# A two-block transformer kernel: x and mem loaded as feature tiles, tap spectra and norm steps in another order, sparse attention's products over all 128 rows

## Chip, core and metric

One core of a Trainium2 chip runs the whole program in one launch. The metric is the device time of one execution in microseconds; times are medians of several runs, and a profile is one further execution.

## What is computed

Two blocks of a model run one after the other on 256 tokens of 1024 features, in float32.

```python
def first_block(x, mem, ...):
    h = x
    h = h + hybrid_mixer(rmsnorm(h, norm_mix_g), ...)      # state-space scan and stick-breaking attention
    h = h + memory_cross_attention(rmsnorm(h, norm_xa_g), mem, norm_mem_g, ...)
    h = h + sqrelu_mlp(rmsnorm(h, norm_ff_g), w_ff1, w_ff2)
    return rmsnorm(h, final_g)

def conformer_conv(h, ...):                                # second block, first layer
    a, gate = jnp.split(h @ w_pw1 + b_pw1, 2, axis=-1)
    u = causal_dwconv_2(a * jax.nn.sigmoid(gate), w_dw, b_dw)   # width 31
    u = jax.nn.silu(layernorm(u, ln_g, ln_b))
    return u @ w_pw2 + b_pw2

def nsa_attention(h, ...):                                 # second block, second layer
    # 16 query heads, 4 key heads of 64; three branches, gated and added:
    # compressed keys (15 blocks), selected blocks, sliding window
    return o @ w_out
```

Each layer of the second block ends in a gated feed-forward net (`conv_ffn`, width 2816). With 256 tokens every block is selected and the window covers everything before a token, so the selected and the window branch are both causal softmax attention with keys of their own.

## The kernel before

Activations lie with features on the partitions: a tile of two feature blocks is 128 partitions by 2 by 256 tokens. Every weight streams once from one long array, in chunks of 128 by 1024 (512 KB), in the order of `_plan`. `chunk` (L351) loads one into one of five `raw` buffers (SP issues the DMA, L348), ScalarE writes `hi`, the rounded fp32r part (L356), and VectorE the rest `lo` (L357); there are seven buffers of each. A product with a weight is three fp32r products: hi by hi, hi by lo, lo by hi (`mm_b`, `mm_a`; all products are issued at L309). Activations are split likewise (`Norm.feed`: ScalarE at L529, VectorE at L530). A product of plain fp32 tiles takes two passes and stands in the profile as two instructions.

The code is straight-line Python. The framework takes each engine's instructions in the written order as far as their operands and buffers are there by its own estimate of times, and adds the waits; so an instruction that is ready may go ahead of one written earlier. Buffers come from pools by tag: `c4` (4 KB a partition, NC4 of them), `t2` (2 KB, eight), PSUM banks `acc` (four), `up` (two), `ms` (two).

**Start.** `load_tokens` (L317) reads mem, and later x, with tokens on the partitions, in four pieces each, the rows of a piece 1 KB long. `turned` (L582) transposes a piece on TensorE (four transposes at L587, PSUM tile `ps_t`), VectorE copies the result (L596 for mem, L609 for x, the latter into `hT`), and `feed` makes the split parts. SP issues in the order mem 0, the first constants `ct`, mem 1, the first vectors `vt`, mem 2, the first chunk of w_xv, mem 3, and further chunks. mem's products come first (w_xv, PSUM `ps_v`, L555), then x is transposed, then w_xk (`ps_xk`, L613), then the mixer's projections.

**Conv module (L974 to L1128).** The depthwise convolution of width 31 is done in the frequency domain: `dft_load` brings matrices and taps, `tap_spectra(m)` (L993) makes the taps' spectra with products over 32 rows (PSUM `ps_sp`, copied by ScalarE at L998), `project` (L1000) makes one 512-wide half of the value (`a`) or gate (`g`) projection out of four chunks (`ps_pw`), `forward` and `back` go to the spectrum and back (`ps_f`, `ps_y`). `normed(t)` (L1061) does the layer norm of 128 tokens: statistics, a reciprocal root, and the scaling of two halves b = 0, 1 of 512 features, b = 1 on VectorE (L1072) and b = 0 on ScalarE (L1074). `feature(p, t)` (L1077) transposes them back (`ps_t`, p = 0, 1 from half 0), `activated` applies silu, and the `pw` products follow.

**Sparse attention (L1170 to L1461).** Its steps are letters in `NSA_ORDER` (L30), written out by hand: p, n, r project, norm and rotate a group of query heads, w makes the softmax weights of a pair of heads (`n_weights`, L1319), t transposes them, c and u do the compressed branch, o forms the output (`n_out`, L1398). Keys are in `kh` (hi, for both halves of the partitions) and `kl` (lo). A query tile `qq` holds hi on the 64 partitions of its own half and lo on the other 64, so one product with `kh` over 128 rows gives hi by hi and lo by hi; the product with `kl` uses 64 rows (L1336). A third, bf16 product adds the mask. VectorE takes the minimum (L1338), ScalarE the exps (L437 in `fn`), GpSimd scales them by gates and sums (L1346). In `n_out` the compressed values `vbd`, of 64 rows for each pair, are multiplied first (L1401), then the two other branches' transposed weights.

Of the kernel before, what the change touches and what calls it, by code (L numbers as in the profile page):

```python
# [16 lines left out]
P = 128  # L17
T = 256
# [6 lines left out]
NEG = -1e30  # L25
NC4 = 7
NT2 = 8
NT1 = 4
FRONT_ORDER = "D0 X2 Z0 Q0 S0 X0 W0 Z1 W1 b0 L0 u2 u4 X1 u1 Q1 u0 Q2 L1 T0 E0 B0 G0 T1 u3 Y0 W4 G1 Y1 y0 b4 W2 W5 Q3 b1 W3 b2 V0 W6 y1 n0 W7 b3 b6 V1 b5 O1 b7 O3 O0 O2 a0 s0 N0 q0 w0 q1 o0 w1 w2 o1 w3 o2 o3"
NSA_ORDER = "W1 K1 W0 R1 G0 K0 H0 g0 p0 h0 R0 H1 n0 r0 C0 p1 n1 w0 h1 V0 w1 V1 c0 t0 r1 c1 p2 C1 u0 t1 n2 w2 u1 c2 w3 o0 p3 r2 w4 t2 o1 n3 u2 t3 w5 r3 o2 w6 o3 t4 c3 w7 t5 t6 o4 o5 u3 t7 o6 o7"  # L30

def _up(w, c0=0, c1=None, cols=None):
    s = w[:, c0:c1] if cols is None else w[:, cols]
    k, n = s.shape
    return s.reshape(k // P, P, n).transpose(1, 0, 2).reshape(P, -1)


# [14 lines left out]
def _plan():  # L54
# [234 lines left out]
def kernel(ctx: ExitStack, tc: tile.TileContext, x: bass.AP, mem: bass.AP, stream: bass.AP,  # L289
# [26 lines left out]

    def load_tokens(src, j):  # L317
        t = spool.tile([P, 2, 256], F32, tag="t2", name="xin", bufs=NT2)
        nc.sync.dma_start(t, src.rearrange("o (t p) d -> p (o t) d", p=P)[:, :, 256 * j:256 * j + 256])
        return t  # L320

    mem_in = [load_tokens(mem, 0)]
    nc.sync.dma_start(ct[:, :first], cons[:, :first])
    mem_in.append(load_tokens(mem, 1))
    nc.sync.dma_start(vt[:, :16], vecs[:, :16])
    mem_in.append(load_tokens(mem, 2))

# [11 lines left out]

    offs, o = {}, 0  # L340
    for key, width, _ in _PLAN:
        offs[key] = (o, width)
        o += P * width

    def raw_chunk(key):
        off, width = offs[key]
        raw = wpool.tile([P, 1024], F32, tag="raw", name="raw", bufs=5)
        nc.sync.dma_start(raw[:, :width], stream[off:off + P * width].rearrange("(p c) -> p c", p=P))  # L348
        return raw, width
# [231 lines left out]

    def turned(t_):  # L582

        ps = acc_bank([P, 2, T], "ps_t")
        for f in range(2):
            for t in range(2):
                pe.transpose(ps[:, f, P * t:P * t + P], t_[:, t, P * f:P * f + P], ident)  # L587
        return ps

    mn = Norm("g_mem", eps1)  # L590
    for j in range(4):
        if j == 1:
            wxv = [chunk(("xv", 0), 256)]
            mem_in += [load_tokens(mem, 3)]
        mT = spool.tile([P, 2, T], F32, tag="t2", name="mT", bufs=NT2)
        dve.tensor_copy(mT, turned(mem_in[j]))  # L596
        mn.feed(j, mT)
    ms_ = mn.xs
# [4 lines left out]
    v_cols("xv", 1, ms_, col, vx)  # L603
    x_in = [load_tokens(x, j) for j in range(4)]
    hT = new_h()
    nm = Norm("g_mix", eps1)
    for j in range(4):
        ps = turned(x_in[j])
        dve.tensor_copy(hT[:, 2 * j:2 * j + 2, :], ps)  # L609
        nm.feed(j, hT[:, 2 * j:2 * j + 2, :])  # L610
# [381 lines left out]

    def tap_spectra(m):  # L993
        for b in range(2):
            s = slice(512 * b, 512 * b + 512)
            ps = (up_bank, ms_bank)[m]([P, 512], "ps_sp")
            mm(ps, cv["raw"][0:32, 768 + P * m:768 + P * m + P], cv["taps"][0:32, s], True, True)
            act.activation(cv["v"][:, m, s], ps, AF.Copy)  # L998

    def project(key):  # L1000

        kind, b = key
        cv[key] = ps = [acc_bank([P, 512], "ps_pw%d" % t) for t in range(2)]
# [12 lines left out]
        if key == ("g", 0):
            cv["col"] = tok_col(nm)
# [43 lines left out]
    def normed(t):  # L1061
# [7 lines left out]
        for b in range(2):  # L1069
            y = spool.tile([P, 512], F32, tag="t2", name="yn", bufs=NT2)  # L1070
            if b:
                dve.tensor_scalar(y, cv["y", b, t], mv[:, 0:1], r[:, 0:1], op0=ALU.subtract, op1=ALU.mult)  # L1072
            else:
                act.activation(y, cv["y", b, t], AF.Identity, scale=r[:, 0:1], bias=r[:, 1:2])  # L1074
            cv["n", b, t] = y
# [19 lines left out]
    project(("a", 0))  # L1095
    for m in range(2):
        tap_spectra(m)
    glu(0)
# [71 lines left out]
    kh = apool.tile([P, 4, 2, T], F32R, tag="b8", name="kh")  # L1170
    kl = apool.tile([P, 2, 2, T], F32R, tag="c4", name="kl", bufs=NC4)
    halves = (slice(0, 64), slice(64, 128))

    def head_norm(src, gain, y, n=2 * T):
# [78 lines left out]
    def key_parts(a):  # L1253
        k = rope(st["y", a])
        for u, r in enumerate(halves):
            act.activation(kh[r, u:4:2, a, :], k[r], AF.Copy)
            dve.tensor_sub(kl[r, :, a, :], k[r], kh[r, u:4:2, a, :].bitcast(F32))
            pool.dma_start(kh[halves[1 - u], u:4:2, a, :], kh[r, u:4:2, a, :])
# [60 lines left out]
    def n_weights(i):  # L1319
# [78 lines left out]
    def n_out(i, pts, ect):  # L1398
        gp, r = i // 4, halves[i % 2]
# [24 lines left out]
    def cmp_values(hv):  # L1424
# [4 lines left out]
        for gp in range(2):  # L1429
# [98 lines left out]
```

## Time and profile before

| what | value |
|---|---|
| runs shown | 1026.71, 1027.13, 1030.53 us (median 1027.13) |
| the profiled execution | 1030.8 us, span from first to last instruction 1028.6 us |
| TensorE products, busy | 1012.2 us (98%), 6651 instructions |
| weight loads into TensorE | 891.0 us (87%) |
| VectorE | 741.2 us (72%) |
| ScalarE | 612.3 us (60%) |
| GpSimd | 43.2 us (4%) |
| DMA | 166.94 MB, 162 GB/s |
| mean granted clock of TensorE | 0.993 |

Busy times overlap and are means over stages with different limits. The granted clock is a share of TensorE's full speed (2.4 GHz); 0.50 is its other level, 1.2 GHz. Ends of products in the profile are modelled, so the distance from one start to the next says more than a duration. "PEld" is the loading of a product's stationary operand.

### The profile page before, as it was taken

How to read it: one execution, taken by the hardware profiler on the slowest of the kernel's cores; microseconds unless marked ns; L12 is line 12 of the kernel's file. 1: busy time of each engine (PE TensorE's matmuls, PEld its weight loads, DVE VectorE, ACT ScalarE, POOL GpSimd, SP SyncE). 2: the span in 40 equal slices, each digit the busy share in tenths (PEclk: the TensorE clock that was granted, in tenths of full speed). 3: DMA queues.
4: the chain of work that ended last, by engine and by line, in shares of the span. 5: the costliest groups of instructions: out<-in, count | busy, mean ns of one | idle time of the engine just before them, and what ended most of it. 6: DMA issues, size and time to landing. Idle time of an engine off the chain costs nothing.

```text
span 1028.6 us, 17279 instructions
## 1 busy us (share of the span) xinstructions
PE 1012.2 (98%) x6651; PEld 891.0 (87%) x6651; DVE 741.2 (72%) x1219; ACT 612.3 (60%) x1083; POOL 43.2 (4%) x128
## 2 busy tenths in 40 slices
PE   7999999999999999989999999999999999999998
PEld 6998899899999997869999998996886898888887
DVE  6977568676566669567987878775887379878784
ACT  6757666655555567456755556654867567555552
POOL 0000000000000000000000000010224200000000
PEclk9999999999999999989999999999999999999999
DMA  8754235266555636614665655456621056555541
GB/s 310 256 185 144 70 96 183 64 218 195 188 176 183 203 112 200 209 42 136 222 196 177 192 183 187 131 175 213 199 93 41 1 160 196 198 187 188 198 144 41
DMA packets 48865, 166.94 MB, mean 162 GB/s; under 512 B 5616, under 2 KB 8560, under 8 KB 48784
## 3 DMA queue, kind: packets, MB, share of 16 engines
q1 hardware_dynamic: 48016, 164.80, 49.3%
q0 software_dynamic: 768, 1.05, 0.5%
q8 instruction: 52, 0.85, 0.3%
q14 instruction: 29, 0.24, 0.1%
HBM read 163.73 MB, written 1.05 MB: 160 GB/s over the span
## 4 chain that ended last, share of the span: by engine, by line
PE 94%; DVE 2%; DMA 2%; ACT 1%; issue 1%; SPq 0%; POOL 0%; DVEq 0%; POOLq 0%; ACTq 0%
PE ps_up L309 24%; PE ff L309 9%; PE ps_ff L309 9%; PE ob L309 6%; PE dn L309 6%; PE ps_pw L309 5%; PE ps_v L309 4%; PE pw L309 2%; PE nl L309 2%; PE ps_qk L309 2%; PE no L309 2%; PE wo L309 2%; PE npo L309 2%; PE ps_xbc L309 2%; PE ps_nq L309 1%; PE zt L309 1%
## 5 line engine op out<-in xcount | busy, mean ns | idle before, releaser
L357 DVE TENSOR_TENSOR lo<-raw,hi 128x1024 fp32r<-128x1024 f32 x296 | 356.4, 1217 | 135.9 <-ACT hi L356 133.7
L356 ACT ACTIVATE hi<-raw 128x1024 fp32r<-128x1024 f32 x296 | 306.1, 1050 | 197.6 <-PE ps_up L309 63.3
L309 PE MATMUL ps_up<-x,hi 128*128 128x512 f32 x704 | 249.2, 398 | 0.0
L309 PE MATMUL ps_up<-x,lo 128*128 128x256 f32 x704 | 198.2, 281 | 0.0
L309 PEld LDWEIGHTS ps_up<-x,hi 128*128 128x128 f32 x704 | 132.3, 188 | 31.7
L309 PEld LDWEIGHTS ps_up<-x,lo 128*128 128x128 f32 x704 | 133.0, 189 | 0.4
L309 PE MATMUL ff<-us,hi 128*128 128x256 f32 x512 | 93.1, 283 | 0.0
L309 PE MATMUL ps_ff<-x,hi 128*128 128x512 f32 x256 | 90.6, 396 | 0.0
L309 PEld LDWEIGHTS ff<-us,hi 128*128 128x128 f32 x512 | 79.4, 190 | 1.1 <-DVE us L472 0.2
L309 PE MATMUL ff<-us,lo 128*128 128x256 f32 x256 | 72.3, 283 | 0.0
L309 PE MATMUL ps_ff<-x,lo 128*128 128x256 f32 x256 | 72.0, 281 | 0.0
L309 PE MATMUL dn<-us,hi 128*128 128x256 f32 x352 | 63.7, 283 | 0.0
L309 PEld LDWEIGHTS ps_ff<-x,hi 128*128 128x128 f32 x256 | 48.1, 188 | 10.7
L309 PE MATMUL ob<-hi,us 128*128 128x512 f32 x176 | 56.0, 391 | 0.0
L309 PEld LDWEIGHTS dn<-us,hi 128*128 128x128 f32 x352 | 54.7, 191 | 0.4
L309 PE MATMUL dn<-us,lo 128*128 128x256 f32 x176 | 49.8, 283 | 0.0
L309 PEld LDWEIGHTS ff<-us,lo 128*128 128x128 f32 x256 | 48.7, 190 | 0.0
L309 PEld LDWEIGHTS ps_ff<-x,lo 128*128 128x128 f32 x256 | 48.4, 189 | 0.0
L309 PE MATMUL ps_pw<-hi,x 128*128 128x512 f32 x128 | 42.9, 411 | 0.0
L1144 DVE SCALAR_TENSOR_TENSOR fc<-fa,vt,fc 128x256 f32<-128x256 f32 x88 | 42.2, 479 | 0.9
L309 PEld LDWEIGHTS ob<-hi,us 128*128 128x128 f32 x176 | 33.0, 188 | 7.3
L309 PE MATMUL ps_v<-hi,x 128*128 128x256 f32 x192 | 38.3, 295 | 0.0
(378 smaller groups left out, 2005.2 us busy)
## 6 DMA issues: line engine op xcount, KB each, us to landing
raw<-in_stream_dram SPq DMA_DIRECT2D x303, 512.0 KB, 4.2
xin<-in_mem_dram SPq DMA_DIRECT2D x4, 256.0 KB, 4.2
xin<-in_x_dram SPq DMA_DIRECT2D x4, 256.0 KB, 4.2
bb<-in_stream_dram SPq DMA_DIRECT2D x4, 256.0 KB, 3.7
out_dram<-htok SPq DMA_DIRECT2D x4, 256.0 KB, 2.0
ct<-in_cons_dram SPq DMA_DIRECT2D x1, 705.0 KB, 8.1
kh<-kh POOLq DMA_DIRECT2D x4, 128.0 KB, 5.1
vt<-in_vecs_dram SPq DMA_DIRECT2D x1, 363.5 KB, 5.3
```

What stands on the lines that cost most here:

```text
L309: pe.matmul(ps, l, r, start=start, stop=stop, skip_group_check=True, **kw)
L356: act.activation(hi[:, :width], raw[:, :width], AF.Copy)
L357: dve.tensor_sub(lo[:, :width], raw[:, :width], hi[:, :width].bitcast(F32))
L1144: dve.scalar_tensor_tensor(c, a[:, k:k + T], vec(wd, 3 * j + k), c, op0=ALU.mult, op1=ALU.add)
```

## The change

- mem and x are laid out on the host as feature tiles and become eight pieces of the stream, 256 KB each, with rows of 2 KB. The transposes and copies go; mem's pieces are fed as loaded, x's pieces are loaded straight into `hT`. The first w_xv chunk is requested behind mem's first piece, the other three pieces behind it. The first vectors and constants are issued by ScalarE. Twelve bf16 products of 512 columns on a cleared tile stand at the very start.
- In the conv module, the four tap products (m, b) stand in `project(("a", 0))`, one ahead of each weight chunk, and all use `up` banks. In `normed`, VectorE takes half 1 for the first token tile and half 0 for the second.
- In sparse attention `kl` becomes two tiles with one cleared half each, and `vbd` two tiles with the other pair's rows cleared, so that both products use all 128 rows. NC4 is 8 instead of 7, the small weight tile `ne0` moves from `c4` to `t2`, and r2 and r3 stand earlier in `NSA_ORDER`.

```diff
-NC4 = 7
+NC4 = 8
-NSA_ORDER = "... u1 c2 w3 o0 p3 r2 w4 t2 o1 n3 u2 t3 w5 r3 o2 ..."
+NSA_ORDER = "... r2 u1 c2 w3 o0 p3 t2 w4 o1 n3 u2 t3 r3 w5 o2 ..."
...
+def _feats(x, j):
+    return x[:, 256 * j:256 * j + 256].reshape(T, 2, P).transpose(2, 1, 0).reshape(P, 2 * T)
...
+    for name in ("mem", "x"):
+        for j in range(4):
+            add((name + "T", j), 512, lambda I, name=name, j=j: _feats(I[name][0], j))
...
+    idle = spool.tile([P, 2, T], BF, tag="t2", name="idle", bufs=NT2)
+    pool.memset(idle, 0.0)
+    pi = psum.tile([P, 2, T], F32, tag="ms", name="pi", bufs=2)
+    for i in range(12):
+        mm(pi, idle[:, 0, 0:P], idle, True, True)
...
+    nc.scalar.dma_start(vt[:, :16], vecs[:, :16])
+    mem_in = [load_tokens("memT", 0)]
...
     mn = Norm("g_mem", eps1)
+    wxv = [chunk(("xv", 0), 256)]
+    nc.scalar.dma_start(ct[:, :first], cons[:, :first])
+    mem_in += [load_tokens("memT", j) for j in range(1, 4)]
+    wxv.append(chunk(("xv", 1), 256))
     for j in range(4):
-        if j == 1:
-            wxv = [chunk(("xv", 0), 256)]
-            mem_in += [load_tokens(mem, 3)]
-        mT = spool.tile([P, 2, T], F32, tag="t2", name="mT", bufs=NT2)
-        dve.tensor_copy(mT, turned(mem_in[j]))
-        mn.feed(j, mT)
+        mn.feed(j, mem_in[j])
...
-    x_in = [load_tokens(x, j) for j in range(4)]
     hT = new_h()
+    for j in range(4):
+        load(hT[:, 2 * j:2 * j + 2, :].rearrange("p a t -> p (a t)"), ("xT", j))
     nm = Norm("g_mix", eps1)
     for j in range(4):
-        ps = turned(x_in[j])
-        dve.tensor_copy(hT[:, 2 * j:2 * j + 2, :], ps)
         nm.feed(j, hT[:, 2 * j:2 * j + 2, :])
...
-    def tap_spectra(m):
-        for b in range(2):
-            s = slice(512 * b, 512 * b + 512)
-            ps = (up_bank, ms_bank)[m]([P, 512], "ps_sp")
-            mm(ps, cv["raw"][0:32, 768 + P * m:768 + P * m + P], cv["taps"][0:32, s], True, True)
-            act.activation(cv["v"][:, m, s], ps, AF.Copy)
+    def tap_spectra(m, b):
+        s = slice(512 * b, 512 * b + 512)
+        ps = up_bank([P, 512], "ps_sp")
+        mm(ps, cv["raw"][0:32, 768 + P * m:768 + P * m + P], cv["taps"][0:32, s], True, True)
+        act.activation(cv["v"][:, m, s], ps, AF.Copy)
...
         for k in range(4):
+            if key == ("a", 0):
+                tap_spectra(*divmod(k, 2))
             w = chunk((key, k), 512)
...
-            if b:
+            if b == 1 - t:
                 dve.tensor_scalar(y, cv["y", b, t], mv[:, 0:1], r[:, 0:1], op0=ALU.subtract, op1=ALU.mult)
...
-    for m in range(2):
-        tap_spectra(m)
     glu(0)
...
-    kl = apool.tile([P, 2, 2, T], F32R, tag="c4", name="kl", bufs=NC4)
+    kl = [apool.tile([P, 2, 2, T], F32R, tag="c4", name="kl%d" % u, bufs=NC4) for u in range(2)]
     halves = (slice(0, 64), slice(64, 128))
+    for u in range(2):
+        pool.memset(kl[u][halves[1 - u]].bitcast(F32), 0.0)
...
-    vbd = spool.tile([P, 2, P], F32, tag="sb_p", name="vbd")
-    for t_ in (kcp, h1v, vbd):
+    vbd = [spool.tile([P, 2, P], F32, tag="sb_p", name="vbd%d" % i) for i in range(2)]
+    for t_ in (kcp, h1v, *vbd):
         pool.memset(t_, 0.0)
...
-            e = apool.tile([P, 2, 2, n], F32, tag="c4", name="ne%d" % t, bufs=NC4)
+            if t == 0:
+                e = spool.tile([P, 2, 2, n], F32, tag="t2", name="ne0", bufs=NT2)
+            else:
+                e = apool.tile([P, 2, 2, n], F32, tag="c4", name="ne1", bufs=NC4)
...
-                r, q = halves[u], qp[:, u, P * t:P * t + P]
+                q = qp[:, u, P * t:P * t + P]
                 mm(lg[u], q, kh[:, 2 * gp + u, :, 0:n], t == 1 or u == 0, False)
-                mm(lg[u], q[r], kl[r, gp, :, 0:n], False, False)
+                mm(lg[u], q, kl[u][:, gp, :, 0:n], False, False)
...
-        mm(po, vbd[r, gp], ect[r], True, False)
+        mm(po, vbd[i % 2][:, gp], ect, True, False)
```

## Rows read from the trace of the kernel before

**Rows 1.** The page: the chain that ended last, shares of the span by engine.
```profile
PE 94%; DVE 2%; DMA 2%; ACT 1%; issue 1%; SPq 0%; POOL 0%; DVEq 0%; POOLq 0%; ACTq 0%
```

**Rows 2.** TensorE, 0 to 28: start, duration, engine, line, tile, count, idle.
```profile
10.72 0.56 PE L309 MATMUL ps_v<-hi,x 128*128 128x256 f32 x1
14.55 0.63 PE L309 MATMUL ps_v<-hi,x 128*128 128x256 f32 x2
14.98 0.41 PE L309 MATMUL ps_v<-lo,x 128*128 128x256 f32 x1
25.86 1.91 PE L587 MATMUL ps_t<-ct,xin 128*128 128x128 f32 x16
```

**Rows 3.** ScalarE, 0 to 28: timeline; groups by line (busy us, mean ns).
```profile
9.24 1.06 ACT L356 ACTIVATE hi<-raw 128x1024 fp32r<-128x1024 f32 x1 [0.75 <-DMA raw<-in_stream_dram]
...
L356 ACT ACTIVATE hi<-raw 128x1024 fp32r<-128x1024 f32 x7 | 7.1, 1050 | 0.9 <-DMA raw<-in_stream_dram 0.7
L529 ACT ACTIVATE x<-mT,vt 128x256 fp32r<-128x256 f32 x8 | 3.6, 500 | 4.9 <-DVE mT L596 4.9
L505 ACT ACTIVATE sq<-mT 128x512 f32<-128x512 f32 x4 | 2.3, 614 | 0.0
```

**Rows 4.** Stretches: PE, PEld, DVE, ACT, POOL busy; clock, DMA share, GB/s.
```profile
20.00:27.00 7.00, 7.00 (x60) 6.85 (x59) 2.60 (x6) 3.62 (x8) 0.29 (x1) 1.00 1.01 402
27.00:34.00 7.00, 7.00 (x61) 7.00 (x60) 7.00 (x14) 6.78 (x15) 0.00 (x0) 1.00 0.34 104
```

**Rows 5.** Tap spectra: TensorE's timeline, then the stretch behind them.
```profile
404.86 4.31 PE L309 MATMUL ps_sp<-taps,raw 32*128 32x512 f32 x8
...
409.10:414.50 5.40, 5.40 (x14) 4.25 (x14) 2.00 (x3) 1.54 (x4) 0.00 (x0) 0.50 0.90 319
```

**Rows 6.** The norm's end: timelines of TensorE, VectorE, ScalarE, and the stretch after.
```profile
452.53 1.97 PE L1083 MATMUL ps_t<-ct,yn 128*128 128x128 f32 x8 [2.65 <-ACT yn L1074]
...
450.50 0.80 DVE L1072 TENSOR_SCALAR yn<-ps_y,bmv,brs 128x512 f32<-128x512 f32 x1
...
450.40 1.28 ACT L433 ACT_TABLE_LOAD   x1
451.70 0.78 ACT L1074 ACTIVATE yn<-ps_y,brs 128x512 f32<-128x512 f32 x1
453.25 1.02 ACT L437 ACTIVATE ya<-ps_t,vt 128x256 f32<-128x256 f32 x2 [0.78 <-PE ps_t L1083]
...
454.60:459.00 4.40, 4.37 (x20) 4.37 (x21) 2.28 (x6) 4.40 (x13) 0.00 (x0) 0.50 0.00 0
```

**Rows 7.** Logits of sparse attention: TensorE's timeline, then its weight loads.
```profile
734.17 0.47 PE L309 MATMUL nl<-kh,qq 128*128 128x512 f32 x1
734.58 0.50 PE L309 MATMUL nl<-kl,qq 64*128 64x512 f32 x1
...
735.05 0.48 PE L309 MATMUL nl<-kh,qq 128*128 128x512 f32 x1
...
734.58 0.18 PEld L309 LDWEIGHTS nl<-kl,qq 64*128 64x128 f32 x1 [0.24 <-issue]
```

**Rows 8.** The chain, 723 to 816, by line, and pieces (start, us).
```profile
by line: PE nl L309 26.9%; PE npo L309 20.4%; PE ps_nq L309 12.8%; PE npt L1384 12.7%; PE ps_v L309 12.3%; PE npc L309 3.8%; PE hms L309 3.6%; PE rot L309 2.8%; PE no L309 1.3%; PE ps_col L309 1.1%; PE npct L1393 1.1%; PE pvc L309 0.9%; PE 
...
747.09 5.81 PE ps_nq L309 x48
772.39 0.86 PE rot L309 x2
799.43 0.63 PE npo L309 x2
```

**Rows 9.** Sparse attention: one stretch, then exps and scalings by line.
```profile
780.00:800.00 20.00, 20.00 (x127) 12.57 (x126) 15.03 (x35) 15.91 (x61) 7.75 (x16) 1.00 0.00 1
...
L437 ACT ACTIVATE ne<-nl,nnm 128x128 f32<-128x128 f32 (+1 forms) x64 | 26.2, 422 | 7.6 <-DVE nnm L1338 5.3 <-POOL ne L1346 0.9 <-PE nl L309 0.9
...
L1346 POOL TENSOR_SCALAR ne<-ne,nsm 128x128 f32<-128x128 f32 (+1 forms) x64 | 32.2, 521 | 61.4 <-DVE nsm L1343 24.4 <-DVE nsm L1342 18.1 <-PE ps_col L309 18.0
```

More of the change, by code (lines that the diff above doesn't have):

```diff
@@ L29 @@
 FRONT_ORDER = "D0 X2 Z0 Q0 S0 X0 W0 Z1 W1 b0 L0 u2 u4 X1 u1 Q1 u0 Q2 L1 T0 E0 B0 G0 T1 u3 Y0 W4 G1 Y1 y0 b4 W2 W5 Q3 b1 W3 b2 V0 W6 y1 n0 W7 b3 b6 V1 b5 O1 b7 O3 O0 O2 a0 s0 N0 q0 w0 q1 o0 w1 w2 o1 w3 o2 o3"
-NSA_ORDER = "W1 K1 W0 R1 G0 K0 H0 g0 p0 h0 R0 H1 n0 r0 C0 p1 n1 w0 h1 V0 w1 V1 c0 t0 r1 c1 p2 C1 u0 t1 n2 w2 u1 c2 w3 o0 p3 r2 w4 t2 o1 n3 u2 t3 w5 r3 o2 w6 o3 t4 c3 w7 t5 t6 o4 o5 u3 t7 o6 o7"
+NSA_ORDER = "W1 K1 W0 R1 G0 K0 H0 g0 p0 h0 R0 H1 n0 r0 C0 p1 n1 w0 h1 V0 w1 V1 c0 t0 r1 c1 p2 C1 u0 t1 n2 w2 r2 u1 c2 w3 o0 p3 t2 w4 o1 n3 u2 t3 r3 w5 o2 w6 o3 t4 c3 w7 t5 t6 o4 o5 u3 t7 o6 o7"
 def _up(w, c0=0, c1=None, cols=None):
@@ L315, with load, load_tokens @@
     first = _COFF["strict"][0]
-    def load_tokens(src, j):
-        t = spool.tile([P, 2, 256], F32, tag="t2", name="xin", bufs=NT2)
-        nc.sync.dma_start(t, src.rearrange("o (t p) d -> p (o t) d", p=P)[:, :, 256 * j:256 * j + 256])
-        return t
[L322 to L326, printed above, removed]
+    idle = spool.tile([P, 2, T], BF, tag="t2", name="idle", bufs=NT2)
[3 more added lines that the diff above has]
+        mm(pi, idle[:, 0, 0:P], idle, True, True)
+    offs, o = {}, 0
+    for key, width, _ in _PLAN:
+        offs[key] = (o, width)
+        o += P * width
+    def load(dst, key):
+        off, width = offs[key]
+        nc.sync.dma_start(dst, stream[off:off + P * width].rearrange("(p c) -> p c", p=P))
+    def load_tokens(name, j):
+        t = spool.tile([P, 2, T], F32, tag="t2", name="xin", bufs=NT2)
+        load(t.rearrange("p a t -> p (a t)"), (name, j))
+        return t
+    nc.scalar.dma_start(vt[:, :16], vecs[:, :16])
+    mem_in = [load_tokens("memT", 0)]
     def con(name):
@@ L337 @@
     eps1, eps2, one, eps12 = (con("eps")[:, i:i + 1] for i in range(4))
[L340 to L343, printed above, removed]
     def raw_chunk(key):
-        off, width = offs[key]
+        width = offs[key][1]
         raw = wpool.tile([P, 1024], F32, tag="raw", name="raw", bufs=5)
-        nc.sync.dma_start(raw[:, :width], stream[off:off + P * width].rearrange("(p c) -> p c", p=P))
+        load(raw[:, :width], key)
         return raw, width
@@ L579, in dump @@
                 nc.sync.dma_start(out[0, P * t:P * t + P, 256 * q:256 * q + 256], ot)
[L582 to L588, printed above, removed]
     mn = Norm("g_mem", eps1)
+    wxv = [chunk(("xv", 0), 256)]
+    nc.scalar.dma_start(ct[:, :first], cons[:, :first])
+    mem_in += [load_tokens("memT", j) for j in range(1, 4)]
+    wxv.append(chunk(("xv", 1), 256))
     for j in range(4):
-        if j == 1:
-            wxv = [chunk(("xv", 0), 256)]
-            mem_in += [load_tokens(mem, 3)]
-        mT = spool.tile([P, 2, T], F32, tag="t2", name="mT", bufs=NT2)
-        dve.tensor_copy(mT, turned(mem_in[j]))
-        mn.feed(j, mT)
+        mn.feed(j, mem_in[j])
     ms_ = mn.xs
@@ L1256, in key_parts @@
             act.activation(kh[r, u:4:2, a, :], k[r], AF.Copy)
-            dve.tensor_sub(kl[r, :, a, :], k[r], kh[r, u:4:2, a, :].bitcast(F32))
+            dve.tensor_sub(kl[u][r, :, a, :], k[r], kh[r, u:4:2, a, :].bitcast(F32))
             pool.dma_start(kh[halves[1 - u], u:4:2, a, :], kh[r, u:4:2, a, :])
@@ L1398, in n_out @@
     def n_out(i, pts, ect):
-        gp, r = i // 4, halves[i % 2]
+        gp = i // 4
         po = ms_bank([P, T], "npo")
-        mm(po, vbd[r, gp], ect[r], True, False)
+        mm(po, vbd[i % 2][:, gp], ect, True, False)
         for t, kt, s in pts:
@@ L1434, in cmp_values @@
             for q in range(4):
-                dve.tensor_copy(vbd[32 * q:32 * q + 32, gp, 64 * (q % 2):64 * (q % 2) + 64], pv[32 * q:32 * q + 32, :])
+                dve.tensor_copy(vbd[q // 2][32 * q:32 * q + 32, gp, 64 * (q % 2):64 * (q % 2) + 64], pv[32 * q:32 * q + 32, :])
     st = {}
```

## The prediction

> **What bounds the kernel now.** I read the chain of work that ended last first: 94% of it is TensorE [rows 1], so what is taken off TensorE's queue is taken off the span, unless another engine stands right behind it, and work taken off VectorE or ScalarE counts only where TensorE waits for it. Then I read the four places the diff touches. In the start (0 to 28 us) TensorE's first product of a weight stands at 10.72 [rows 2]; the weight landed at 9.24 [rows 3]. Two products of 256 columns there take 0.43 us (14.55 to 14.98), 0.215 each [rows 2], where one at the full level takes 5.81 / 48 = 0.121 [rows 8]; so I read the half level, 1.2 GHz, out of the durations, up to about 15.2. In the conv module two stretches have a granted clock of 0.50: 409.1 to 414.5, behind eight passes of the tap spectra on 32 rows [rows 5], and 454.6 to 459.0, behind transposes that waited 2.65 us for a normed tile [rows 6]. In sparse attention (723 to 816) the logits (nl) alone are 26.9% of the chain, 25.0 us [rows 8].
>
> The profiled execution took 1030.8 (span 1028.6, 2.2 around it); the runs shown are 1026.71, 1027.13 and 1030.53. All sums below are against 1030.8, 3.7 above the median. The stretch at the taps costs about that much (3.5, below), so the median run may lack one of the two that the profile has.
>
> **Start: x and mem as feature tiles.** Removed are the transposes of mem and x and their PSUM copies on VectorE; 16 passes of x's transposes alone hold TensorE from 25.86 for 1.91 us [rows 2]. Added are a cleared tile, 12 bf16 products of 512 columns on it, and two small loads issued from ScalarE instead of SP. The 12 wait for one GpSimd memset only and last at most 12 x 0.43 = 5.2 us (twice the 0.215 of 256 columns, at the half level). They end before a weight can be there, so I cost them at nothing; what they may bring is that the first real products run at 0.121.
> Moved: the first w_xv chunk is issued second on SP instead of sixth, with 0.26 MB ahead of it instead of 0.92. At the 402 GB/s of a saturated stretch [rows 4] the 0.66 MB less are 1.6 us, and four issue slots of some 0.5 us (an estimate) are 2.0; so it lands near 9.24 - 3.4 = 5.8. hi takes 1.05 [rows 3] and lo on VectorE about as long, so dense products start near 8.2, and 96 of them at 0.121 end at 19.8.
> What is late next is ScalarE. Until the first two w_xk chunks are converted it has 8 mem feeds (3.6 us), 4 squares (2.3), 4 conversions for w_xv (4.2), scaling and rows (some 2.6, an estimate by the 0.5 of a feed), 8 x feeds (4.0) and 2 conversions (2.1), 18.8 us by the means of [rows 3]; from about 2.8 on, when mem's first tile may be there (an estimate), that ends near 21.6. Both of its added DMA issues lie before that, while it has nothing landed. Today w_xk starts at about 27.6, after the transposes [rows 2]. So 27.6 - 21.6 = **6.0 us**. Bounds: 7.8 if only TensorE's work counts (19.8), 1.9 if just the transposes go. DMA would allow it: it runs at 402 GB/s from 20 to 27, then idles at a share of 0.34 until 34 [rows 4], as I read it because the raw buffers are full; earlier consumption frees these sooner.
>
> **Conv: the four tap products spread between the weights of project(a, 0).** The same eight passes stay, but take 4.31 us today [rows 5] where at the 0.43 of a 512-column fp32 pass (0.86 / 2, rot) [rows 8] they would take 3.44: the last ones are already slowed. They stand between full-row products now, and I expect the clock to stay up: saved are these 0.8 and half of the 5.4 us at 0.50 behind them, 2.7. Against it: each product on 32 rows now meets a change of rows on both sides, which on 64 rows costs about 0.2 a side at most (below): I take 0.1 for each of four. **3.0 us**; bounds -0.8 (the clock falls all the same, 0.2 each) and 3.5. The four copies of their results on ScalarE stay.
>
> **Conv: the norm's halves.** For the second token tile the first half now goes to VectorE, which has a 0.80 us slot at 450.50; today ScalarE makes that half at 451.70, behind a table load (450.40), until 452.5, and TensorE's transposes start at 452.53 [rows 6]. They could start at 451.3, but the silu behind them still waits for ScalarE to end its own half at 452.5 instead of starting at 453.25. So 0.75: **0.8 us** at the first product of pw (454.6). Whether that keeps the clock up I leave open: if so, half of 454.6 to 459.0, 2.2, comes on top; I take 0 since transposes and an idle TensorE remain there. Bounds 0 and 3.0.
>
> **Sparse attention: products over all rows.** In a group of 512 columns the 128-row product (kh) starts at 734.17, the 64-row one (kl) at 734.58 and the next kh, behind the bf16 mask, at 735.05 [rows 7]: 0.88 a group. At the steady rate, 0.121 per 256 columns [rows 8], it would be 0.24 + 0.24 + 0.12 = 0.60. The difference lies around the 64-row product: its weight load (0.18) starts only with its product, idle 0.24 before [rows 7]; so the load is not hidden behind the product before it. 16 groups of 512 columns at 0.60 and 16 of 256 at 0.36 are 15.4; today they are 25.0. Saved: 9.6. The compressed values' product takes 0.63 on 64 rows [rows 8]; two passes of 512 columns on 128 rows take 0.86 there (rot), so 256 columns 0.43: 8 x 0.2 = 1.6. Together 11.2 us of TensorE.
> The rest of the edit costs other queues: two memsets of a half tile and one more of vbd on GpSimd, ahead of its two key DMAs but early, while it is idle; SBUF room: kl takes two c4 slots instead of one (8 of them now instead of 7), while the small tile ne0 goes to t2, so that three ne1 fit where three tiles of both kinds did. The query ropes move two steps earlier.
> How much of 11.2 stays is bounded by the others: ScalarE is busy 15.91 of 20 us and VectorE 15.03 from 780 to 800 [rows 9]; with a share of 11.2 x 20 / 93 = 2.4 us less that is 15.9 of 17.6, and more where logits stand close. The additional slots let a head be prepared earlier, where there is room. I take three quarters, **8.4 us**; bounds 1 and 11.2.
> The Trainium skill, page "TensorE: Matmul & The Clock Gate", sections "LDWEIGHTS (loading the stationary operand)" and "Why this matters for your kernels", says that the row count does not matter for a weight load and that a product on few rows takes as long as on all; by that rule this edit would bring nothing. The load's own length agrees (0.18 here); its place does not.
>
> **Sum.** 6.0 + 3.0 + 0.8 + 8.4 = 18.2, so 1030.8 - 18.2 = 1012.6; against the median, which may lack the 3.5 of one clock stretch, 1027.1 - 18.2 + 3.5 = 1012.4 or, if it lacks none, 1008.9. I say **1011**.
>
> **Rivals.**
> A, given back in sparse attention: ScalarE and the chain of a head (reduce, exp, scale, transpose, copy) become the bound; 1 instead of 8.4: 1020.0. For it speaks 15.91 of 20 [rows 9], against it that the chain of 723 to 816 names lines of TensorE alone, 99.7% of it [rows 8].
> B, the change does not do what it says to the clock: zeros do not raise it at the start (2.2 less, half of 10.72 to 15.2) and the taps still drop it (-0.8 instead of 3.0): 1012.6 + 6.0 = 1018.6.
> C, the start is bound by loads or ScalarE all the same: 1.9 instead of 6.0: 1016.7. For it speaks the 402 GB/s, against it the idle DMA right behind.
> D, the exposed 0.2 us do not come from the rows but from the order of fp32r and bf16 products in one bank: 0 instead of 8.4: 1021.0. This is also what the page's rule would give. Against it: 48 fp32r products in one bank at 0.121.
> E, slower: ne0 now takes one of the 8 t2 slots that raw queries, rope halves and three copies per head share, and a head's exps wait until the head before is out. Then heads go in series: products 1.9, eight exps at 0.42 (3.4), eight scalings on GpSimd at 0.52 (4.2) [rows 9], copies, output and accumulator reads some 4.5 (an estimate): 14.0 a head against 93 / 8 - 1.4 = 10.2 of TensorE work. 3.8 x 8 = 30 us lost, less 18.2: 1043. It decides from 18.2 / 8 = 2.3 us of added wait per head. Against it: a ne0 is dead after the first four transposes of its head.
>
> **How the numbers follow.** Forecast 0.66 (its own range 1004 to 1017, by the bounds: all upper ends 1030.8 - 25.5 = 1005, one at its lower end and the rest as taken up to 1017), A 0.12, B 0.08, C 0.07, D 0.03, E 0.04. Range 1003 to 1020 holds forecast, most of A, B and C. A measurement of this kernel tells 0.5%, 5.1 us, from no change. Faster by more (below 1022): all but E and pairs of A to D: 0.92; within: 0.04; slower: 0.04.
>
> **What would show it.** Start: no ps_t, first w_xv products at 0.12 us, w_xk before 23. Conv: granted clock 1.00 through project(a, 0) and project(g, 1); pw starting about 0.8 sooner after the last ps_y. Sparse attention: nl groups of 0.60 and 0.36 us, all 128 rows, and 723 to 816 shorter by 8 us with TensorE never idle. I am wrong if TensorE waits for ne or nps there, if granted clock is 0.50 after the taps, or if weight products before 30 us wait for hi.

## The result, and the profile after

The changed kernel takes 1018.1 us (median of four, 1016.27 to 1019.77) where the kernel before takes 1026.92 on the same chip: ratio 0.9902, interval 0.9878 to 0.9925. Taken again on another chip (e9_after_again below) it was 0.9892, 0.987 to 0.9913. The kernel before has another median on each chip used here (1026.9, 1028.4, 1029.1, 1030.6), so kernels are compared by their ratio, or with kernels timed beside them on the same chip. By the ratio the gain is 10 to 11 us (the two medians alone differ by 8.8 here and by 12.3 on the other chip), where the sum on record had 18.2. The time lies in the range of 1003 to 1020, 7 above the 1011 that was said, and above the forecast's own range, which ended at 1017.

The profiled execution took 1019.77 (span 1018.0), against 1030.8 before: 11.0 less, 10.6 of them in the span. The page's first part, busy time by engine, shows that TensorE is still busy for 98% of the span:

```profile
PE 1002.1 (98%) x6631; PEld 883.5 (87%) x6631; DVE 735.5 (72%) x1211; ACT 611.3 (60%) x1083; POOL 48.3 (5%) x132
```

To see where the 10.6 came from, I set the starts of the same products in the two traces side by side:

| product | before | after | gain so far |
|---|---|---|---|
| first `ps_xk` | 27.52 | 22.37 | 5.2 |
| last `ff`, ahead of the conv module | 380.65 | 375.39 | 5.3 |
| last `ps_pw` (conv projections) | 433.38 | 426.06 | 7.3 |
| first `pw` (behind the norm) | 454.63 | 446.43 | 8.2 |
| last `pw` | 479.59 | 470.43 | 9.2 |
| last `pz` (ahead of sparse attention) | 712.48 | 704.27 | 8.2 |
| last `ps_nq` (its last query projection) | 772.10 | 759.73 | 12.4 |
| last `no` (its output) | 838.00 | 827.41 | 10.6 |
| last `ob` (end) | 1024.47 | 1013.89 | 10.6 |

So start 5.2 (6.0 was said), taps 2.1 (3.0), norm 0.9 and another 0.9 to 1.0 that is lost again before `pz`, sparse attention 2.4 (8.4): 10.6. Of the 7.6 that are missing, 6.0 are missing from sparse attention. It had won 4.2 us up to `ps_nq`, and 1.8 of them go again.

**Start**, TensorE's timeline (start, duration, line, tile, count, idle before), which answers [rows 2]:

```profile
1.31 4.53 PE L317 MATMUL pi<-idle 128*128 128x512 bf16 x12 [1.31 <-POOL idle L327]
6.10 0.39 PE L317 MATMUL ps_v<-hi,x 128*128 128x256 f32 x1 [0.26 <-ACT x L545]
7.11 0.38 PE L317 MATMUL ps_v<-lo,x 128*128 128x256 f32 x1 [0.63 <-DVE lo L373]
7.50 0.50 PE L317 MATMUL ps_v<-hi,x 128*128 128x256 f32 x2
7.84 0.28 PE L317 MATMUL ps_v<-lo,x 128*128 128x256 f32 x1
7.96 0.32 PE L317 MATMUL ps_v<-hi,x 128*128 128x256 f32 x1
```

and its waits from 0 to 30 (engine, line, releaser: us in total, times, longest), with one stretch (length; busy us of PE, PEld, DVE, ACT, POOL; granted clock; DMA share; GB/s):

```profile
PE ps_v L317 <- DVE lo L373: 1.5, 2, 0.9
PE pi L317 <- POOL idle L327: 1.3, 1, 1.3
PE ps_v L317 <- ACT hi L372: 0.9, 1, 0.9
...
10.00:15.00 5.00, 3.27 (x26) 2.87 (x25) 4.54 (x7) 5.00 (x9) 0.00 (x0) 1.00 1.05 406
```

From 7.84 to 7.96 a product takes 0.12, and the first one starts 4.6 us sooner than before. But TensorE waits for the split weights, 2.4 us in three pieces: from 10 to 15 ScalarE, which makes `hi`, is busy without a break and TensorE is not.

**Conv**, stretches, columns as above, which answer [rows 5, 6]; the last is in sparse attention:

```profile
404.00:409.00 5.00, 5.00 (x24) 4.14 (x23) 5.00 (x8) 2.87 (x4) 0.00 (x0) 1.00 0.83 297
409.10:414.50 5.40, 5.40 (x25) 4.47 (x24) 3.18 (x4) 2.54 (x3) 0.00 (x0) 1.00 0.95 330
...
445.30:448.60 3.30, 3.20 (x14) 2.80 (x15) 1.43 (x4) 3.30 (x10) 0.00 (x0) 0.50 0.00 0
...
769.60:776.30 6.70, 6.37 (x18) 3.80 (x19) 2.74 (x8) 3.67 (x11) 3.23 (x8) 0.50 0.19 71
```

The stretch at 0.50 (1.2 GHz) behind the taps is gone, the one behind the norm is 3.4 us long instead of 6.8, and there is a new one of 6.8 in sparse attention. At the norm TensorE's idle 2.65 of [rows 6] is now 1.48 and 0.52:

```profile
444.04 0.66 PE L1090 MATMUL ps_t<-ct,yn 128*128 128x128 f32 x4 [1.48 <-DVE yn L1079]
445.21 1.11 PE L1090 MATMUL ps_t<-ct,yn 128*128 128x128 f32 x4 [0.52 <-ACT yn L1081]
446.43 0.79 PE L317 MATMUL pw<-x,hi 128*128 128x256 f32 x2
```

**Sparse attention.** The logits' groups, in answer to [rows 7], go from one `kh` to the next in 743.84 - 743.25 = 0.59 us where they took 0.88. The last row is the weight load of the `kl` product, now on 128 rows. It starts 0.23 ahead of its product, while the `kh` product runs; on 64 rows it started together with its product (734.58 in [rows 7]):

```profile
743.25 0.48 PE L317 MATMUL nl<-kh,qq 128*128 128x512 f32 x1
743.56 0.40 PE L317 MATMUL nl<-kl,qq 128*128 128x512 f32 x1
743.80 0.28 PE L317 MATMUL nl<-cmb,identb 128*128 128x256 bf16 x1
743.84 0.47 PE L317 MATMUL nl<-kh,qq 128*128 128x512 f32 x1
...
743.33 0.19 PEld L317 LDWEIGHTS nl<-kl,qq 128*128 128x128 f32 x1
```

What gives the gain back is a wait that the kernel before doesn't have. ScalarE's waits, 710 to 806, the longest first, then what they do in the timelines of TensorE, ScalarE and GpSimd:

```profile
ACT ne L453 <- PE npo L317: 6.2, 2, 3.2
```

```profile
757.27 1.58 PE L317 MATMUL npo<-nps,vn 128*64 128x128 f32 x24
...
758.89 0.37 ACT L453 ACTIVATE ne<-nl,nnm 128x128 f32<-128x128 f32 x1 [3.17 <-PE npo L317]
780.67 0.37 ACT L453 ACTIVATE ne<-nl,nnm 128x128 f32<-128x128 f32 x1 [3.07 <-PE npo L317]
...
764.89 4.63 POOL L1356 TENSOR_SCALAR ne<-ne,nsm 128x128 f32<-128x128 f32 x8 [3.91 <-DVE nsm L1353]
...
768.66 1.38 PE L1394 MATMUL npt<-ct,ne 128*128 128x128 f32 x3 [0.86 <-POOL ne L1356]
```

The first exponential of a pair writes ne0, now in one of the eight t2 buffers. It starts at 758.89, just when a run of output products (757.27 + 1.58 = 758.85) has read copied weights (`nps`) for the last time. Of what these products read, `nps` alone lies in a t2 buffer, so it is a buffer of `nps` that ne0 had been handed. These are the first output products of the stage, and the exponentials are those of the fourth pair: in `NSA_ORDER` w3 stands ahead of o0, so they wait for an output that TensorE comes to later. At 780.67 the sixth pair's (w5) wait likewise for the third output (o2). After the first wait the sums, GpSimd's scalings (until 769.5) and the transposes that TensorE meets at 768.66 are then late by that much, and behind the idle TensorE the clock falls (769.6 to 776.3).

### The profile page after: what moved, and what is told of

Read it like the earlier page. It is cut to its first block, busy times and chain, and to the rows that moved or that the text cites. A ratio compares the mean times of both kernels' runs of the same rounds, so it can differ in the third digit from the quotient of the medians.

```text
span 1018.0 us, 17221 instructions
## 1 busy us (share of the span) xinstructions
PE 1002.1 (98%) x6631; PEld 883.5 (87%) x6631; DVE 735.5 (72%) x1211; ACT 611.3 (60%) x1083; POOL 48.3 (5%) x132
## 5 line engine op out<-in xcount | busy, mean ns | idle before, releaser
L317 PEld LDWEIGHTS ps_ff<-x,hi 128*128 128x128 f32 x256 | 48.1, 188 | 10.6
```

Of the source, the lines that this page charges most:

```text
L317: pe.matmul(ps, l, r, start=start, stop=stop, skip_group_check=True, **kw)
```

## The experiments

Each with its edit, what was expected and what came. All were timed against the kernel before on the same chip: e1 to e4 on one, e5 to e8 on a second, e9 to e12 on a third.

| run | median us | before | ratio, interval | mean granted clock of its executions |
|---|---|---|---|---|
| e1_start | 1022.88 | 1028.38 | 0.9947, 0.9931 to 0.9963 | 0.993 to 0.998 |
| e2_conv | 1027.57 | 1028.38 | 0.9993, 0.9977 to 1.0009 | 0.997 to 1.0 |
| e3_attn | 1026.91 | 1028.38 | 0.9984, 0.9966 to 1.0002 | 0.990 to 0.996 |
| e4_ne0_own | 1011.62 | 1028.38 | 0.9844, 0.9823 to 0.9865 | 0.998 to 0.999 |
| e5_own_rows64 | 1021.74 | 1029.13 | 0.9928, 0.9905 to 0.9951 | 0.997 to 0.999 |
| e6_own_one_idle | 1012.18 | 1029.13 | 0.9834, 0.9811 to 0.9858 | 0.998 to 1.0 |
| e7_own_old_order | 1011.64 | 1029.13 | 0.9826, 0.9803 to 0.9849 | 0.998 to 1.0 |
| e8_own_taps_old | 1012.64 | 1029.13 | 0.9844, 0.9819 to 0.9868 | 0.992 to 1.0 |
| e9_after_again | 1018.28 | 1030.58 | 0.9892, 0.987 to 0.9913 | 0.996 to 0.999 |
| e10_own_norm_old | 1012.83 | 1030.58 | 0.9835, 0.9814 to 0.9855 | 0.997 to 0.998 |
| e11_half_own | 1014.7 | 1030.58 | 0.9854, 0.9834 to 0.9875 | 0.997 to 0.998 |
| e12_two_edits | 1014.44 | 1030.58 | 0.9851, 0.983 to 0.9873 | 0.995 to 0.997 |

### One part at a time: e1_start, e2_conv, e3_attn

The kernel before with the edits of the diff to the start alone (tiles, idle products, loads), to the conv module alone (taps and norm halves), to sparse attention alone.

> The kernel before with the start of the change alone: x and mem as feature tiles, the twelve idle products, the loads in their new order; convolution and sparse attention as before. Theory (the parts add up, and the start is worth what the two traces show of it): the first w_xk product starts near 22.4 instead of 27.5 us, 5.2 us come through unchanged to the end, 1021.7 us. Rival (time won at the start is partly lost where the clock falls later or a load is met sooner): under 4 us, above 1023. The prediction on record had 6.0, which would be 1021.

Measured: 0.0053 x 1028.4 = 5.5 us (3.8 to 7.1), `ps_xk` first at 21.89. The part carries its gain to the end by itself; the theory holds.

> The kernel before with the convolution part alone: one taps product ahead of each weight chunk of project(a, 0), and ScalarE and VectorE exchanged for the halves of the second layer norm. Theory: the clock no longer falls at 407.8 us (2.1 us), the norm's halves end 0.9 us sooner and the stretch at half clock behind them is 3.4 us instead of 6.8 (another 0.9): 3.9 us in all, 1023.0. The prediction on record had 3.0 + 0.8, 1023.1. Rival (the shorter stretch behind the norm is chance of where the clock's change fell, or a fall of the clock elsewhere takes it back): 2 to 3 us, 1024 to 1025.

Measured: 0.7 us (0.9 lost to 2.4 won), less than either theory. Its trace has the shorter stretches at half clock, and the executions of this kernel run at a mean clock of 0.997 to 1.0; yet the time hardly moves. The next run shows one reason.

> The kernel before with sparse attention's part alone: kl and vbd on all 128 rows, ne0 in a t2 buffer, the new order. Theory (the products gain, but ne0 in t2 waits for output products, transposes wait behind it and the clock falls): the products between 723 and 772 us gain about 4.2 us, the second half gives it back, and 1 to 2.5 us are left, 1024.5 to 1026. Rival (the sum on record: three quarters of 11.2 us stay): 8.4 us, 1018.5. If the loss needs the earlier edits, it is this that shows it.

Measured: 1.6 us (0.2 lost to 3.5 won), the gain that the theory left; the loss needs no other edit. ScalarE waits 6.2 us for `npo` here too, TensorE is at half clock from 775.4 to 782.3. Its conv module is that of the kernel before, instruction for instruction, but in this execution the clock did not fall at the taps. TensorE's timeline, then the stretch behind:

```profile
404.26 3.70 PE L309 MATMUL ps_sp<-taps,raw 32*128 32x512 f32 x8
...
408.00:414.40 6.40, 6.40 (x29) 5.26 (x30) 3.67 (x4) 3.71 (x6) 0.00 (x0) 1.00 0.95 371
```

So the fall of [rows 5] is not in every execution. The projections with the taps in their midst, in this trace and in that of e2_conv, in which they are spread (min/median/max ns, first and last start):

```profile
L309 PE MATMUL ps_pw<-hi,x x128: 387/389/579, 380.2 to 429.6; 128*128 128x512 f32 x128
```

```profile
L309 PE MATMUL ps_pw<-hi,x x128: 387/389/577, 380.3 to 430.8; 128*128 128x512 f32 x128
```

49.4 us with the eight together, 50.5 spread, both at full clock; before, with the fall, 433.38 - 380.77 = 52.6. Spreading costs 1.1 and saves 3.2 when the clock would have fallen, 2.1 on balance.

### Where sparse attention's gain goes: e4_ne0_own

```diff
-                e = spool.tile([P, 2, 2, n], F32, tag="t2", name="ne0", bufs=NT2)
+                e = spool.tile([P, 2, 2, n], F32, tag=("bb", "xpad")[i % 2], name="ne0", bufs=2)
```

The tags bb and xpad belong to stages that are over by then.

> The changed kernel with ne0 in buffers of its own, two that are not in use at that time (those of bb and xpad in turn), instead of one of the eight t2 buffers. Nothing else is changed. Theory (the t2 buffers are the loss): ScalarE's two exponentials that wait 6.2 us in sum for an output product (758.9 and 780.7 us) wait no more, the transposes of the fourth pair don't wait for GpSimd near 768 us, TensorE stays at full clock there, and 3.4 us of clock plus up to 2.6 us of waits come back: 1012 to 1015. Rival (ScalarE and GpSimd can't deliver faster, whatever the buffers): the waits move to another releaser, the clock falls as before, 1017 to 1019. Third (two buffers for eight pairs are themselves too few, the next ne0 waits for the transposes of the pair two before): slower than the changed kernel, above 1019.

Measured: 0.9844, 16.0 us under the kernel before: 5 to 6 better than the changed kernel (10 to 11). ScalarE's waits from 710 to 806 name no `npo` for `ne` any more, the longest of `ne` is

```profile
ACT ne L453 <- DVE nnm L1348: 4.2, 5, 1.5
```

The whole stage, from the last `pz` to the last `npo`, as one stretch; the changed kernel's first, then e4_ne0_own's:

```profile
704.20:806.20 102.00, 98.21 (x752) 78.39 (x746) 77.12 (x176) 75.32 (x212) 35.90 (x68) 0.97 0.33 107
```

```profile
702.40:796.70 94.30, 92.85 (x750) 75.62 (x746) 76.63 (x176) 74.38 (x212) 35.47 (x68) 1.00 0.35 115
```

102.0 against 94.3 us. TensorE's idle falls from 3.8 to 1.5, the granted clock is 1.00 instead of 0.97 (half of the 6.8 us, 3.4), and 2.0 of the 7.7 are left for products that stand less densely (shares of this pair of executions; e9_after_again has others). Up to the last `ps_nq` both kernels have gained the same 4.2 us on the kernel before; behind it e4_ne0_own gains 5.9 more, where the changed kernel loses 1.8. From `pz` to the last `no` this kernel gains 20.1 - 10.0 = 10.1 us on the kernel before, where the changed one gains 2.4. ScalarE's and VectorE's work is the same as before and fits into the shorter stage (74.4 and 76.6 of 94.3): the rival of throughput falls, and so does the third.

### The rows alone: e5_own_rows64

```diff
-                mm(lg[u], q, kl[u][:, gp, :, 0:n], False, False)
+                mm(lg[u], q[halves[u]], kl[u][halves[u], gp, :, 0:n], False, False)
-        mm(po, vbd[i % 2][:, gp], ect, True, False)
+        mm(po, vbd[i % 2][halves[i % 2], gp], ect[halves[i % 2]], True, False)
```

> The kernel of e4_ne0_own (no stretch at half clock in it) with the products of kl and of vbd on 64 of the 128 rows again; tiles, buffers and order stay. It prices the rows alone. Theory of the prediction on record (each of the products of fewer rows costs 0.1 to 0.2 us more beside those of 128): the 512-column groups of the scores go from 0.59 back to about 0.88 us, the output products from 0.52 to 0.63, and the whole loses between 8 and 11 us against e4_ne0_own, 1019 to 1023. Rival (the row count costs nothing, the gain of that part came from the order and the buffers): within 2 us of e4_ne0_own, 1010 to 1014.

Measured: 1021.74, 9.1 to 10.1 above e6 to e8 on the same chip. The groups are back at 746.13 - 745.25 = 0.88, and the weight load of the 64-row product starts with its product again:

```profile
745.25 0.48 PE L317 MATMUL nl<-kh,qq 128*128 128x512 f32 x1
745.66 0.50 PE L317 MATMUL nl<-kl,qq 64*128 64x512 f32 x1
746.09 0.28 PE L317 MATMUL nl<-cmb,identb 128*128 128x256 bf16 x1
746.13 0.48 PE L317 MATMUL nl<-kh,qq 128*128 128x512 f32 x1
...
745.66 0.18 PEld L317 LDWEIGHTS nl<-kl,qq 64*128 64x128 f32 x1 [0.25 <-issue]
```

Rows, then, not order or buffers. The Trainium skill, page "TensorE: Matmul & The Clock Gate", section "LDWEIGHTS (loading the stationary operand)", says that a weight load of few rows takes as long as one of 128. The lengths agree (0.18 us here, 0.19 in the changed kernel); what differs, along with the 0.29 us of a group, is when the load starts.

### The idle products: e6_own_one_idle

```diff
-    for i in range(12):
+    for i in range(1):
         mm(pi, idle[:, 0, 0:P], idle, True, True)
```

> The kernel of e4_ne0_own with one idle product at the start instead of twelve. Theory (the idle products bring the clock's full level ahead of the first w_xv product): the clock record begins its full level later than 4 us, the first products at half clock take twice their 0.12, and w_xk starts 1 to 3 us later than 21.9, 1013 to 1015. Rival (the start is bound by loads and by ScalarE and VectorE anyway, the removed transposes alone gave the 5.2 us): w_xk starts at 21.9 within 0.5 us, 1011 to 1012.

Measured: 1012.18, beside 1011.64 and 1012.64, and `ps_xk` starts at 22.48 instead of 21.94: 0.55 us. That is hardly more than executions differ: with twelve idle products it starts from 21.84 to 22.37 in ten traces. The mechanism is as the theory has it, its price is not. The products at the start do run at half the rate, from 7.1 to 12.8 us (busy us, mean ns of one, idle before):

```profile
L317 PE MATMUL ps_v<-hi,x 128*128 128x256 f32 x16 | 5.2, 426 | 0.0
L317 PE MATMUL ps_v<-lo,x 128*128 128x256 f32 x9 | 3.9, 433 | 0.4 <-DVE lo L373 0.4
```

In those 5.7 us TensorE is busy 5.68 with 25 products, in e4_ne0_own 4.38 with 29: at full clock it does a little more and then waits for `hi` and `lo`. The waits take up most of what the clock gives.

### The order and the taps: e7_own_old_order, e8_own_taps_old

e7, in `NSA_ORDER`, and then e8:

```diff
-w2 r2 u1 c2 w3 o0 p3 t2 w4 o1 n3 u2 t3 r3 w5
+w2 u1 c2 w3 o0 p3 r2 w4 t2 o1 n3 u2 t3 w5 r3
```

```diff
-            if key == ("a", 0):
-                tap_spectra(*divmod(k, 2))
...
     project(("a", 0))
+    for k in range(4):
+        tap_spectra(*divmod(k, 2))
```

> The kernel of e4_ne0_own with sparse attention's steps in the order of the kernel before (r2, t2, r3 back in their places). Theory (the new order's earlier r2 and t2 are needed so that products don't stand behind a late rope or weights): TensorE meets a wait of 1 to 3 us near 760 to 790 us, 1013 to 1016. Rival (with ne0 off the t2 buffers the order is indifferent): 1011 to 1012.5, no new wait over 0.5 us.

Measured: 1011.64, no wait of TensorE over 0.3 us in the stage. The new order is worth nothing that shows here: the rival.

> The kernel of e4_ne0_own with the eight taps products together behind project(a, 0) again. The trace of e3_attn, whose convolution is that of the kernel before, shows no fall of the clock there, and its products of ps_pw end 1.2 us sooner than where they are spread (gain 3.2 against 2.1 us). Theory A (spreading them only insures against a fall of the clock that comes in some executions, and costs about 1 us in itself): 1011 to 1012.5, a lower bottom and a wider spread than e4_ne0_own, clock 0.996 to 0.999. Theory B (the prediction on record: the eight together bring the clock down in every execution, 3 us): 1014 to 1015, clock 0.996 or less in every execution.

Measured: median 1012.64, executions from 1010.99 (clock 1.0) over 1013.59 (0.994) to 1017.92 (0.992). Mostly theory A, though 0.5 to 1.0 above e6 and e7: the bottom is as low as with the taps spread, the spread wider. In the profiled one the clock had fallen:

```profile
404.00:407.90 3.90, 3.90 (x8) 2.48 (x8) 1.31 (x2) 0.89 (x2) 0.00 (x0) 0.50 0.62 200
```

Over all traces of this study: with the eight together the clock fell there in four of five (6.8 us long in the kernel before, in e1_start and here, 3.4 in e12_two_edits, not in e3_attn), spread in none of nine.

### Controls and halves: e9_after_again, e10_own_norm_old, e11_half_own, e12_two_edits

e9 is the changed kernel. e10 is e4_ne0_own with the first of these edits, e11 the changed kernel with the second:

```diff
-            if b == 1 - t:
+            if b:
...
-                e = spool.tile([P, 2, 2, n], F32, tag="t2", name="ne0", bufs=NT2)
+                tag, bufs = (("bb", "xpad")[i % 2], 2) if i < 4 else ("t2", NT2)
+                e = spool.tile([P, 2, 2, n], F32, tag=tag, name="ne0", bufs=bufs)
```

e12 is e4_ne0_own with taps, their PSUM banks, norm halves and `NSA_ORDER` as before.

> The changed kernel unaltered, beside the others of this call, so that its distance from the kernels with ne0 in other buffers is taken on one chip. Theory (the first measurement holds): 0.990 of the kernel before, 1017 to 1020, clock 0.994 to 0.998; the exponentials' waits for output products (6.2 us) are there again, whether or not the clock falls near 770 us. Rival (that measurement was lucky or unlucky by a stretch at half clock): 1014 or 1022.

Measured: 1018.28, as expected, with the waits:

```profile
ACT ne L453 <- PE npo L317: 6.5, 2, 3.3
```

In this trace the stretch at half clock in sparse attention is only 3.4 us (771.1 to 774.5) and TensorE idles 4.8 us in the stage instead of 3.8; its gain at the end is the same 10.6. And one execution at a mean clock of 0.999 took 1017.78, another at 0.996 took 1017.66. So the fall of the clock is a companion of the loss; what it adds beyond the waits these runs don't separate.

> The kernel of e4_ne0_own with ScalarE and VectorE of the second layer norm's halves as in the kernel before. It prices the exchange alone. Theory (it moved TensorE's wait there from 2.65 us in one piece to 1.5 and 0.5, gain 0.6 to 0.9 and sometimes half a stretch of half clock with it): 1012 to 1014, one idle of 2.6 us ahead of the second set of transposes. Rival (nothing that a measurement can tell): 1011 to 1012.5.

Measured: 1012.83, ratio 0.9835 beside 0.9844 for e4_ne0_own: nothing that a measurement can tell, though its trace has the idle of 2.6 us in one piece and 6.8 us at half clock behind it.

> The changed kernel with ne0 of the first four pairs in buffers of their own and of the last four in t2 again. It asks where the t2 buffers cost. Theory 1 (the wait at 758.9 us is the one that lets the fourth pair's weights come late and the clock fall): the wait of 3.2 us there is gone, the one near 780 stays, the clock doesn't fall near 770, 1012 to 1014.5. Theory 2 (the second wait costs as much): 1014.5 to 1017. Rival (it isn't the buffers but the amount of work that moved): 1017 to 1019.

Measured: 1014.7, 3.6 under e9_after_again and 1.9 above e10_own_norm_old. It falls just above theory 1, at theory 2's edge: both waits cost. One is left, and with it a wait of TensorE for GpSimd's scalings (0.9):

```profile
ACT ne L453 <- PE npo L317: 3.3, 1, 3.3
```

The clock didn't fall in its sparse attention (1.00 over the stage), and yet it is slower than with none of the waits: the wait that is left costs without the clock.

> The kernel before with only the two edits that the runs so far show to pay: the start, and the products over all 128 rows with ne0 in buffers of its own. Convolution, norm and the order of sparse attention are as before. Theory (the conv module's edits and the new order are worth nothing that the median shows): 1011 to 1013.5, the bottom as low as e4_ne0_own's 1010.6, the spread wider, because the clock falls at the taps in some executions. Rival (each is worth what the prediction on record gave it, 3.0 + 0.8): 1015 to 1016.

Measured: 1014.44, 1.6 above e10_own_norm_old, between the two. The two edits carry 15.4 of the 16 to 18 us; what the taps and the order add is at most 1 to 2. Its bottom, 1013.2, isn't as low as that of e10_own_norm_old (1011.95), at clocks of 0.995 to 0.997.

**A version that beats both kernels** is e4_ne0_own, with either order: 0.9844 and 0.9826 of the kernel before.

## Why the prediction was right or wrong, point by point

**The total** lies in the stated range, but that range had been drawn wide enough for rivals A, B and C; the forecast's own range, 1004 to 1017, is missed by 1.1, and three of the four parts came out short. That 1018.1 stands next to B's 1018.6 is chance: B's mechanism did not occur. Two of the recorded signs of being wrong were there. Weight products waited for `hi` before 30 us, and in sparse attention TensorE waited for `nps` and `ne` (700 to 812):

```profile
PE npt L1394 <- ACT nps L1396: 1.1, 2, 0.8
PE npt L1394 <- POOL ne L1356: 0.9, 1, 0.9
```

**The bound** was right: TensorE is busy 98% of the span in both kernels, and each microsecond taken off its queue in the start came through (5.2 at `ps_xk`, 5.3 at `ff`, and 5.5 in the time of e1_start).

**Start, 6.0: measured 5.2**, within its bounds (the old start begins `ps_xk` from 26.96 to 27.52 in the traces at hand, so 5.2 stands for 4.6 to 5.7). Idle products cost nothing, the first weight products run near 0.12, `ps_xk` starts before 23. What was mis-sized is the chain behind it. ScalarE's conversions were to be what is late, until 21.6; they end at 20.81:

```profile
19.76 1.05 ACT L372 ACTIVATE hi<-raw 128x1024 fp32r<-128x1024 f32 x1
```

TensorE's dense products were to end at 19.8; they reach `ps_xk` at 22.37 without a wait there, having waited 2.4 us for `hi` and `lo` earlier, 1.7 of them behind 8.2, while ScalarE is busy all the time from 10 to 15 (5.00 of 5.00). Rival C holds in part: the start is held up by the conversions, but the gain is 5.2 and not C's 1.9. For that reason the clock's own share was some 0.5 (e6_own_one_idle), where rival B priced it at 2.2.

**Taps, 3.0: measured 2.1 between the profiles, about 1 between kernels** (e8_own_taps_old against e6 and e7, 0.5 to 1.0; e2_conv 0.7), too little to be told from none. The clock stays up, as said. Two steps failed. The change of rows was taken at 0.1 for each of four places and is 1.1 / 4 = 0.28. And the fall was taken from one execution as if each had it. A list of the clocks, which was not yet there, would have warned: of the 24 executions of the kernel before beside e1 to e4, those at a mean clock of 0.998 took 1025.5 to 1028.2, those at 0.992 to 0.993 took 1029.9 to 1031.6, and the profiled one (1030.8, 0.993) was of the latter. The prediction saw that the median may lack a stretch, but still counted the whole of it as saved.

**Norm, 0.8: measured 0.9** at the first `pw`, by the mechanism named: the transposes wait 1.48 and 0.52 instead of 2.65. Over all traces it is 0.6 to 0.9: from the last `ps_pw` to the first `pw` go 21.0 to 21.3 us in the five with the halves as before and 20.4 in the nine others. Half of the stretch at 0.50 went as well in this pair (6.8 to 3.4 us, 0.9 to 1.0), which was left open. With the halves as before it is 6.8 in three traces and 3.4 in two; with them exchanged it is 3.4 in eight and none in one. That second gain was lost at the keys' rotation, where TensorE now waits (0.7 before):

```profile
PE rot L317 <- DVE kr L1189: 1.6, 1, 1.6
```

So 0.9 stays between the profiles, and by e10_own_norm_old it is too little to be seen in the time.

**Sparse attention, 8.4: measured 2.4.** Here the forecast failed, though not where it looked for trouble. The saving itself was counted nearly right: groups of 0.59 us where 0.60 was forecast, 10.1 us in e4_ne0_own of the 11.2 counted, 9.1 to 10.1 in e5_own_rows64. The term that was too large is that of the compressed values' products, 8 x 0.2: where such a product (two passes) stands ahead of the other output products it goes from 0.63 to 0.53, so 0.1 each. Nor were ScalarE and GpSimd the bound, for which a quarter had been held back. The step that failed is the last sentence of rival E: "Against it: a ne0 is dead after the first four transposes of its head". That says when ne0's buffer is given up, and the question was when it is got. The t2 buffer that it was handed had held `nps`, which lives until the output products; with w3 ahead of o0 in the hand-written order, the exponentials wait for products that TensorE has not come to. The other error in E was to price it as all heads in series or none. It came twice in eight pairs, 3.1 to 3.2 us each, and took 7.7 of 10.1. E's point of decision, 2.3 us per pair (E says head), is the point at which the whole change loses; it hid that 7.7 / 8 = 1.0 us per pair already takes most of this part's gain.

**The rivals.** A has the right place and nearly the right time (1020.0 said, 1018.1 measured), but the reason is not its own: e4_ne0_own leaves ScalarE's work as it is and gains 16.0 on the kernel before. B fell: the record of the full level begins at 4.9 us, and no fall followed the taps. C holds in part. D fell with e5_own_rows64, where order and banks stay and only the rows differ. E had the mechanism, the shared buffers, and not the price.

## What to carry to other kernels

When a tile moves into a pool that other tiles share, ask which tile's last reader releases the buffer that it will be handed, and where that reader stands in the queue of its engine; when the new tile dies is the lesser question. Before a stall or a slow clock seen in one profile is counted as a saving, look whether the other executions have it: their times beside their mean clocks tell that. And a product on half the rows between products on all rows can cost more than the same product padded with zeros.

## What the runs showed of the hardware that was not expected

- The same instructions meet a fall of the clock in one execution and not in another: at the taps, with the eight products together, 6.8 us at 0.50 in three traces, 3.4 in one and none in one.
- The profile's clock column can read 1.00 where TensorE runs at the lower level. In e6_own_one_idle it does from 7.1 to 12.8 us, while three products of 256 columns take 0.64 us (8.11 to 8.75), 0.21 each; the record of the clock begins only at 13.1. Ahead of it durations tell the clock, and the column doesn't:

```profile
7.10:12.80 5.70, 5.68 (x25) 5.58 (x26) 5.60 (x12) 5.70 (x12) 0.00 (x0) 1.00 1.03 401
```

- Products on zeros raise the clock as others do: with twelve of them from 1.31 to 5.84 the record of the full level begins at 4.92, and in the ten traces with such a start from 3.95 to 7.09. With one of them (e6_own_one_idle) it begins at 13.14, with none at 14.66 and 15.28; in e3_attn, also with none, at 7.44, and the clock falls again from 10.85 to 14.26.
